# Second feed-forward and MLP by a seven-product block scheme over tokens and rows, with weight sums made by adding loads

## Chip, cores, metric

One core of a Trainium2 chip runs the whole kernel in one launch. The metric is device time in microseconds; a run is one execution, and the time given is a median over runs.

## What is computed

Two transformer blocks follow each other on 512 tokens of 1024 features, in float32. The two parts that the change touches are, cut from the reference:

```python
def swiglu(h, w_gu, w_down):            # first block, second feed-forward: w2_gu, w2_down, D_FF = 2816
    a, b = jnp.split(h @ w_gu, 2, axis=-1)
    return (jax.nn.silu(a) * b) @ w_down

h = modulate(rms_norm(x, g_ffn2[l]), sh3, sc3)
x = x + 0.5 * gt3[:, None, :] * swiglu(h, w2_gu[l], w2_down[l])

def squared_relu_mlp(xn, w_up, w_down): # second block, last part: w_up 1024 x 4096, w_down 4096 x 1024
    return jnp.square(jax.nn.relu(xn @ w_up)) @ w_down

x = x + squared_relu_mlp(rmsnorm(x, norm_mlp[l]), w_up[l], w_down[l])
```

Around them stand a first feed-forward, two mixers and a cross-attention.

## The kernel before

**Layout.** Activations are kept with features on the 128 partitions and the 512 tokens along a row: `x` and `h` are 8 tiles of 128 x 512. Weights are loaded from memory in pieces of 128 x 1024 float32 (512 KB) that the host has laid out in the order of use.

**Products in three passes.** Each float32 operand is split into a rounded part `hi` and a rest `lo`. `new_weights` (line 144) takes a raw piece from a ring of `N_RAW` = 4 buffers, makes `hi` on ScalarE (L151, a copy) and `lo` on VectorE (L152, a subtraction) in a ring of `N_WHL` = 6 `whl` buffers. `mm3` (line 156; the matmul is L160) then issues hi·hi, hi·lo and lo·hi for each row tile into one bank. `split_x` (L203, L204) does the same for activations, which live in a pool of 61 tiles of 128 x 512.

**Stages.** `linear` (line 166) makes one block of 128 columns for all 512 tokens: 8 row tiles, so 24 matmuls with 512 moving columns. `ffn` (line 609) calls it twice for each of 22 tiles of the hidden layer (gate and up), applies tanh and two multiplications (L617 to L619), splits the result into `G`, and between groups of up products runs `down` over 6 tiles of `G` (18 matmuls and one residual addition, L212, for each of the 8 output tiles). `mlp` (line 1251) does so for 32 tiles with L1258 and a square, and with `down` over 8, 8, 6 and 6 tiles (L211). The last 4 tiles go through `res_halves` (line 223), token half by token half with 256 moving columns, so that the next norm can start. The first products of a stage are also done in two token halves (`nhalf`).

**What sets the order.** The text is unrolled; a planner orders each engine's instructions before the run, by their place in the text (earlier is more urgent), by when its own model has their inputs ready, and by when a buffer is free. On the chip each engine takes its list in order, with semaphores. Loads are on SP's queue (L137), each due when a `raw` buffer comes free. There are 8 banks: 6 for `ps()`, 2 for `psx()`. `FIRST` names the weight pieces of the next stage, of which `N_AHEAD` = 1 is split ahead. GpSimd (POOL) does some memsets and issues no loads.

## Time and profile before

| | us |
|---|---|
| runs (3) | 2134.97, 2133.66, 2133.18; median 2133.66 |
| profiled execution | 2137.62 |
| its span, on which all rows stand | 2135.8 |
| granted clock of TensorE, mean | 0.996 |

The page's engines: PE is TensorE's matmuls, PEld its weight loads, DVE VectorE, ACT ScalarE, POOL GpSimd, SP the engine that issues the loads. The ends of matmuls are modelled, so a matmul's pace is read as a stretch divided by the count, not from its mean duration.

### The profile page before, as it was taken

The page shows a single profiled execution, that of the slowest core. Times are in us where ns is not written, and L with a number is a line of the kernel's source. Part 1 is how long each engine was busy: PE and PEld are TensorE (multiplying, and loading weights), DVE is VectorE, ACT ScalarE, POOL GpSimd, SP SyncE. Part 2 cuts the span into 40 slices and gives each one's busy share as a digit, 9 for nine tenths or more (in the row PEclk, how much of TensorE's full clock was granted, in tenths as well). Part 3 has the DMA queues.
Part 4 walks back from the last instruction along what each step waited for, and adds up shares of the span by engine and source line. Part 5 has one row for each costly group of instructions (what it writes and reads, how often), then busy time and mean ns, then how long its engine had stood idle before and what let it go on. Part 6 is the DMA issues. An engine that isn't in the chain of part 4 may idle for free.

```text
span 2135.8 us, 28122 instructions
## 1 busy us (share of the span) xinstructions
PE 2108.9 (99%) x10866; PEld 1767.4 (83%) x10866; DVE 1285.3 (60%) x2644; ACT 802.1 (38%) x1396; POOL 3.7 (0%) x14
## 2 busy tenths in 40 slices
PE   7999999999999999999999999999999999999998
PEld 6888888897777788898888889788889898888887
DVE  6866656588766333473434349889798565343445
ACT  4422222256554322242222225446554444232222
POOL 0000000000000000000000000000000000000000
PEclk9999999999999999999999999999999999999999
DMA  8855555444322233432423232231232313332321
GB/s 303 288 182 186 168 174 166 134 143 130 119 61 79 89 94 94 138 96 72 118 74 112 82 122 81 78 109 40 70 99 82 117 57 102 90 98 81 97 89 40
DMA packets 80278, 243.03 MB, mean 114 GB/s; under 512 B 9104, under 2 KB 14864, under 8 KB 80144
## 3 DMA queue, kind: packets, MB, share of 16 engines
q1 hardware_dynamic: 75536, 234.94, 35.3%
q10 hardware_dynamic: 4608, 6.29, 0.8%
q8 instruction: 86, 1.41, 0.3%
q14 instruction: 48, 0.39, 0.1%
HBM read 232.81 MB, written 8.39 MB: 113 GB/s over the span
## 4 chain that ended last, share of the span: by engine, by line
PE 96%; DVE 2%; ACT 1%; DMA 1%; issue 0%; SPq 0%; DVEq 0%; ACTq 0%
PE p L160 86%; PE x L979 1%; PE p L595 1%; PE x L160 1%; PE x L935 1%; PE x L745 1%; PE x L1037 1%; PE p L602 1%; PE x L920 1%; PE x L734 1%; PE x L302 1%; PE x L322 0%; DMA raw<-in_w_ada 0%; PE x L703 0%; DMA a<-in_memT 0%; ACT a L647 0%
## 5 line engine op out<-in xcount | busy, mean ns | idle before, releaser
L160 PE MATMUL p<-a,whl 128*128 128x512 f32 (+1 forms) x8736 | 1852.2, 371 | 3.3 <-ACT a L557 1.7
L160 PEld LDWEIGHTS p<-a,whl 128*128 128x128 f32 x8736 | 1504.1, 188 | 302.5 <-issue 8.0
L151 ACT CAST whl<-raw 128x1024 fp32r<-128x1024 f32 (+1 forms) x354 | 356.8, 1010 | 762.8 <-PE p L160 551.0
L152 DVE TENSOR_TENSOR whl<-raw,whl 128x1024 fp32r<-128x1024 f32 (+1 forms) x354 | 416.1, 1176 | 152.7 <-ACT whl L151 151.5
L212 DVE SCALAR_TENSOR_TENSOR a<-p,mods,a 128x512 f32<-128x512 f32 (+1 forms) x104 | 64.2, 625 | 83.8 <-PE p L160 83.5
L211 DVE TENSOR_TENSOR a<-a,p 128x512 f32<-128x512 f32 (+1 forms) x96 | 52.4, 553 | 100.5 <-PE p L160 100.2
L618 DVE SCALAR_TENSOR_TENSOR a<-a,p 128x512 f32<-128x512 f32 x44 | 30.2, 687 | 98.3 <-ACT a L617 98.3
L617 ACT ACTIVATE a<-p 128x512 f32<-128x512 f32 x44 | 26.3, 598 | 166.2 <-PE p L160 166.2
L619 DVE TENSOR_TENSOR a<-a,p 128x512 f32<-128x512 f32 x44 | 30.3, 688 | 92.5 <-PE p L160 92.2
L204 DVE TENSOR_TENSOR a<-a 128x512 fp32r<-128x512 f32 x109 | 74.7, 688 | 9.7 <-ACT a L203 9.6
L160 PE MATMUL p<-whl,a 128*128 128x256 f32 (+1 forms) x576 | 75.9, 286 | 0.0
L203 ACT CAST a<-a 128x512 fp32r<-128x512 f32 x109 | 67.0, 618 | 18.3 <-DVE a L1187 6.8
L160 PEld LDWEIGHTS p<-whl,a 128*128 128x128 f32 x576 | 71.3, 188 | 2.6 <-issue 2.2
L1258 DVE SCALAR_TENSOR_TENSOR a<-p,a 128x512 f32<-128x512 f32 x32 | 22.1, 692 | 84.5 <-PE p L160 84.5
L289 ACT ACTIVATE q<-a 128x256 f32<-128x256 f32 x120 | 48.5, 414 | 59.4 <-DVE a L211 28.3
L502 DVE CUSTOM_DVE_ANT_0 raw<-raw,a,ct 128x512 f32<-128x512 f32 x56 | 42.0, 750 | 38.1 <-DMA raw<-in_w_ada 37.4
L291 DVE TENSOR_TENSOR q<-q 128x256 f32<-128x256 f32 x90 | 37.8, 421 | 8.5 <-ACT q L289 7.4
L502 DVE CUSTOM_DVE_ANT_0 raw<-raw,a,part 128x512 f32<-128x512 f32 x56 | 42.0, 750 | 1.2
L722 ACT ACTIVATE a<-a,s 128x256 f32<-128x256 f32 (+1 forms) x64 | 30.0, 470 | 21.2 <-DVE s L717 12.5
L595 PE MATMUL p<-a,raw 128*128 128x256 f32 x80 | 21.6, 426 | 11.8 <-ACT a L549 11.8
L1013 DVE TENSOR_TENSOR a<-a 128x256 f32<-128x256 f32 x64 | 26.4, 419 | 7.2 <-PE x L967 7.1
L1012 ACT COPY a<-a 128x256 f32<-128x256 f32 x64 | 24.7, 411 | 13.3 <-DVE a L1014 12.1
(233 smaller groups left out, 1340.0 us busy)
## 6 DMA issues: line engine op xcount, KB each, us to landing
raw<-in_w_gu SPq DMA_DIRECT2D x88, 512.0 KB, 3.7
raw<-in_w_in SPq DMA_DIRECT2D x86, 512.0 KB, 3.6
raw<-in_w_ada SPq DMA_DIRECT2D x56, 512.0 KB, 4.1
raw<-in_w_down SPq DMA_DIRECT2D x64, 384.0 KB, 3.0
raw<-in_w_up SPq DMA_DIRECT2D x32, 512.0 KB, 3.5
raw<-in_w_down SPq DMA_DIRECT2D x28, 512.0 KB, 3.5
a<-in_w_ada SPq DMA_DIRECT2D x32, 256.0 KB, 4.9
raw<-in_w_out SPq DMA_DIRECT2D x16, 512.0 KB, 3.5
```

Of the source, the lines that this page charges most:

```text
L151: self.nc.scalar.copy(hi[:, ks, :], src)
L152: self.nc.vector.tensor_sub(lo[:, ks, :], src, hi[:, ks, :].bitcast(F32))
L160: self.nc.tensor.matmul(out, lw[k][a], rx[k][b], start=k == 0 and i == 0, stop=k == n - 1 and i == 2)
L203: self.nc.scalar.copy(hi, src)
L204: self.nc.vector.tensor_sub(lo, src, hi.bitcast(F32))
L211: return self.nc.vector.tensor_add(x, x, p)
L212: return self.nc.vector.scalar_tensor_tensor(x, p, gt(j), x, ALU.mult, ALU.add)
L289: nc.scalar.activation(q, x[k], AF.Square, scale=s)
L291: nc.vector.tensor_add(q, accs[i][0], q)
L502: nc.vector.tensor_tensor_reduce(out=t, in0=t, in1=self.cact[i], op0=ALU.mult, op1=ALU.add, scale=0.5, scalar=acc, accum_out=dst)
L595: nc.tensor.matmul(p, w[k], full[k], start=k == 0, stop=k == KT - 1)
L619: nc.vector.tensor_mul(th, th, pb)
```

## The change

In the second feed-forward and the MLP the products with the up weights are done on two by two blocks: rows of the weights in two halves (4 row tiles each), tokens in two halves of 256, and two column groups `c1` and `c2` of 256. Seven products of 128x128 weights with 256 moving columns replace the eight that the plain way needs. `twist` makes the sums of halves of `h` once a stage and splits them; in part they overwrite the second token half of `h`. The sums of weight blocks are made in the raw buffer: `load_q` loads a block of 4 row tiles by 256 columns on SP, and `add_q` lets GpSimd issue a load that adds another block to it, after the buffer has been split for the product before. Signs are carried so that only additions of weights are needed. `unit` holds 4 banks, and its last product is returned to be issued later, inside the next unit (`before`) or in `down` (`between`). The down products go through `res_full` over 4 tiles of `G` (2 in the last group of the feed-forward). The first 2 (feed-forward) or 4 (MLP) hidden tiles are still made by `linear`. The ring of raw buffers gets 5 entries and the pieces shrink from 1088 to 1024 columns, for which the 272-column pieces of the second mixer are cut into four.

```diff
-N_RAW = 4
+N_RAW = 5
...
-    "mix2": [("w_in_2", 0, 4, 3840, 272), ("w_in_2", 512, 4, 3840, 272), ("w_in_2", 0, 4, 3584, 256)],
+    "mix2": [("w_in_2", 0, 2, 3840, 272), ("w_in_2", 256, 2, 3840, 272), ("w_in_2", 512, 2, 3840, 272)],
...
+    def load_q(self, *q):
+        t = self.rawp.tile([128, 1024], F32, tag="raw", name="raw")[:, 0:1024]
+        self.nc.sync.dma_start(t, self.quarter(*q))
+        return t
+
+    def add_q(self, t, *q):
+        self.nc.gpsimd.dma_start(t, self.quarter(*q), accum_op=ALU.add)
+
+    def split_q(self, src):
+        t = self.whlp.tile([128, 2, 1024], F32R, tag="whl", name="whl")
+        hi, lo = (t[:, i, 0:1024] for i in range(2))
+        self.nc.scalar.copy(hi, src)
+        self.nc.vector.tensor_sub(lo, src, hi.bitcast(F32))
+        hi, lo = (u.rearrange("p (k c) -> p k c", k=4) for u in (hi, lo))
+        return [(hi[:, k, :], lo[:, k, :]) for k in range(4)]
+
+    def twist(self, h):
+        nc = self.nc
+        t1, n2, t3, t4 = [], [], [], []
+        a = slice(0, 256)
+        b = slice(256, 512)
+
+        def part(hi, lo, src, sl=slice(0, S)):
+            nc.scalar.copy(hi[:, sl], src)
+            nc.vector.tensor_sub(lo[:, sl], src, hi[:, sl].bitcast(F32))
+            return hi[:, sl], lo[:, sl]
+        for k in range(4):
+            f1, f2, w1, w2 = (self.T() for _ in range(4))
+            for f, (hi, lo) in ((f1, h[k]), (f2, h[k + 4])):
+                nc.vector.tensor_add(f, hi.bitcast(F32), lo.bitcast(F32))
+            nc.vector.tensor_sub(w2[:, a], f1[:, a], f1[:, b])
+            t1.append(part(h[k][0], h[k][1], w2[:, a], b))
+            nc.vector.scalar_tensor_tensor(w1[:, a], w2[:, a], -1.0, f2[:, b], ALU.mult, ALU.subtract)
+            nc.vector.tensor_sub(w1[:, b], f2[:, b], f1[:, b])
+            nc.vector.scalar_tensor_tensor(w2[:, b], w1[:, a], -1.0, f2[:, a], ALU.mult, ALU.subtract)
+            hi, lo = part(self.T(F32R), self.T(F32R), w1)
+            n2.append((hi[:, a], lo[:, a]))
+            t3.append((hi[:, b], lo[:, b]))
+            if k % 2 == 0:
+                q = self.T(F32R), self.T(F32R)
+            t4.append(part(q[0], q[1], w2[:, b], (a, b)[k % 2]))
+        return self.cut(h[0:4], 0, 256), self.cut(h[4:8], 0, 256), self.cut(h[4:8], 256, 512), t1, n2, t3, t4
+
+    def product(self, bank, w, x, first=False):
+        for i in range(2):
+            for k in range(4):
+                for n, (a, b) in enumerate(((0, 0), (0, 1), (1, 0))):
+                    self.nc.tensor.matmul(bank[:, i * 256:i * 256 + 256], w[k][a][:, i * 128:i * 128 + 128], x[k][b],
+                                          start=first and i == 0 and k == 0 and n == 0, stop=k == 3 and n == 2,
+                                          skip_group_check=True)
+
+    def unit(self, name, c1, c2, tw, evac, before):
+        nc = self.nc
+        b11, b21, b22, t1, n2, t3, t4 = tw
+        y = self.load_q(name, 0, c1)
+        A, B, C, D4 = self.ps(), self.ps(), None, None
+        self.product(A, self.split_q(y), b11, True)
+        self.add_q(y, name, 0, c2)
+        s = self.T()
+        nc.scalar.copy(s, A)
+        z = self.load_q(name, 512, c1)
+        self.product(B, self.split_q(z), b21, True)
+        nc.vector.tensor_add(s, s, B)
+        evac(0, 0, s)
+        x = self.load_q(name, 512, c2)
+        D4 = self.ps()
+        self.product(D4, self.split_q(x), t4, True)
+        self.add_q(x, name, 0, c2)
+        C = self.ps()
+        self.product(C, self.split_q(x), t1, True)
+        self.add_q(x, name, 0, c1)
+        self.product(A, self.split_q(x), n2)
+        self.add_q(x, name, 512, c1)
+        u2 = self.T()
+        nc.scalar.copy(u2, A)
+        if before:
+            before()
+        self.product(A, self.split_q(y), t3)
+        u3, n21 = self.T(), self.T()
+        nc.scalar.copy(u3, A)
+        nc.vector.tensor_add(n21, u3, D4)
+        evac(1, 0, n21)
+        nc.vector.tensor_add(u3, u3, C)
+        evac(1, 1, u3)
+
+        def last():
+            self.product(C, self.split_q(x), b22)
+            nc.vector.tensor_add(u2, u2, C)
+            evac(0, 1, u2)
+        return last
...
-    def res_full(self, name, r0, g, gt, c=None):
-        for c0 in range(0, D, 256) if c is None else [c]:
-            wt = self.weights(name, r0, 4, c0, 256)
-            for i in range(0, 256, 128):
+    def res_full(self, name, r0, g, gt, c=None, between=None):
+        n = 1024 // len(g)
+        for c0 in range(0, D, n) if c is None else [c]:
+            wt = self.weights(name, r0, len(g), c0, n)
+            for i in range(0, n, 128):
...
+                if between:
+                    between()
+                    between = None
...
+    def ffn_blocks(self, h, wgu, wdown, gt, after):
...
+        tw = self.twist(h)
...
+            def evac(blk, hf, t):
+                if blk == 0:
+                    th = self.T()
+                    nc.scalar.activation(th, t, AF.Tanh, scale=0.5)
+                    nc.vector.scalar_tensor_tensor(t, th, 1.0, t, ALU.add, ALU.mult)
+                part[blk, hf] = t
+                if (1 - blk, hf) not in part:
+                    return
+                t, n = part.pop((0, hf)), part.pop((1, hf))
+                nc.vector.scalar_tensor_tensor(t, t, -1.0, n, ALU.mult, ALU.mult)
+                self.split_pair(G, f, hf, t)
...
+        for f in range(2, 22, 2):
+            late = self.unit(wgu, f * 128, D_FF + f * 128, tw, evac_of(f), late)
+            n = {4: 4, 8: 4, 12: 4, 16: 4, 20: 2}.get(f, 0)
+            if n:
+                down(done, n, late)
+                done, late = done + n, None
...
-        for f0, nf in ((0, 8), (8, 8), (16, 6), (22, 6), (28, 4)):
...
+        for f in range(4):
+            up(f)
+        tw = self.twist(h)
+        for f in range(4, 32, 4):
+            late = self.unit("w_up_2", f * 128, f * 128 + 256, tw, evac_of(f), None)
+            self.res_full("w_down_2", (f - 4) * 128, [G.pop(i) for i in range(f - 4, f)], None, None, late)
```

`split_pair` splits each 256-column half of a bank into `hi` and `lo` of two tiles of `G`, so four small copies and subtractions take the place of two large ones. In the MLP, `evac` is the comparison with zero and the scaling on VectorE (a minimum with zero for the negated block) and the square on ScalarE.

## Rows read from the trace of the kernel before

**Rows 1.** The page of the kernel before: busy time, share of the span and instructions of each engine, and the chain of work that ended last, by engine and by line (shares of the span).

```profile
PE 2108.9 (99%) x10866; PEld 1767.4 (83%) x10866; DVE 1285.3 (60%) x2644; ACT 802.1 (38%) x1396; POOL 3.7 (0%) x14
PE 96%; DVE 2%; ACT 1%; DMA 1%; issue 0%; SPq 0%; DVEq 0%; ACTq 0%
PE p L160 86%; PE x L979 1%; PE p L595 1%; PE x L160 1%; PE x L935 1%; PE x L745 1%; PE x L1037 1%; PE p L602 1%; PE x L920 1%; PE x L734 1%; PE x L302 1%; PE x L322 0%; DMA raw<-in_w_ada 0%; PE x L703 0%; DMA a<-in_memT 0%; ACT a L647 0%
```

**Rows 2.** Busy time of each engine, the instructions in brackets, in two stretches: the second feed-forward (938 to 1288 us) and the MLP (1771 to 2112). After the engines: granted clock, share of the 16 DMA engines, GB/s.

```profile
core 0: us, PE busy (x) PEld busy (x) DVE busy (x) ACT busy (x) POOL busy (x), PEclk, DMA share, GB/s
938.00:1288.00 350.00, 350.00 (x1643) 289.09 (x1642) 154.67 (x201) 101.02 (x144) 1.43 (x6) 1.00 0.32 96
1771.00:2112.00 341.00, 341.00 (x1547) 279.35 (x1545) 142.75 (x173) 101.62 (x135) 0.00 (x0) 1.00 0.28 85
```

**Rows 3.** Who waited for whom in the MLP's stretch: us in total, times, longest.

```profile
ACT whl L151 <- PE p L160: 224.4, 62, 4.7
DVE a L1258 <- PE p L160: 84.5, 31, 3.3
```

**Rows 4.** The same for SP's queue of loads, over the whole span.

```profile
SPq L137 <- DVE whl L152: 1470.8, 289, 27.8
```

**Rows 5.** Busy time by stretch (columns as in rows 2): 200 us inside the second feed-forward in which all matmuls have 512 moving columns.

```profile
1000.00:1200.00 200.00, 200.00 (x864) 161.74 (x863) 80.50 (x92) 50.66 (x64) 0.00 (x0) 1.00 0.32 95
```

**Rows 6.** The same for the matmuls of line 160 alone (us, PE, PEld, clock, DMA share, GB/s), in two stretches in which all of them have 256 moving columns.

```profile
core 0: us, PE busy (x) PEld busy (x), PEclk, DMA share, GB/s
921.20:931.90 10.70, 10.70 (x90) 10.67 (x91) 1.00 0.35 117
...
1754.20:1763.80 9.60, 9.60 (x81) 9.60 (x81) 1.00 0.34 109
```

**Rows 7.** Groups of instructions in the stretch of rows 5, shapes kept apart: line, engine, operation, tiles, shapes, count, busy us, mean ns of one, idle time before and what ended it.

```profile
L152 DVE TENSOR_TENSOR whl<-raw,whl 128x1024 fp32r<-128x1024 f32 x24 | 29.4, 1226 | 8.3 <-ACT whl L151 8.3
L151 ACT CAST whl<-raw 128x1024 fp32r<-128x1024 f32 x24 | 25.2, 1049 | 62.1 <-PE p L160 45.8 <-issue 16.3
L212 DVE SCALAR_TENSOR_TENSOR a<-p,mods,a 128x512 f32<-128x512 f32 x16 | 12.0, 751 | 30.9 <-PE p L160 30.9
L618 DVE SCALAR_TENSOR_TENSOR a<-a,p 128x512 f32<-128x512 f32 x12 | 8.3, 689 | 42.3 <-ACT a L617 42.3
L619 DVE TENSOR_TENSOR a<-a,p 128x512 f32<-128x512 f32 x12 | 8.3, 688 | 36.3 <-PE p L160 36.3
L204 DVE TENSOR_TENSOR a<-a 128x512 fp32r<-128x512 f32 x12 | 8.2, 685 | 0.0
L617 ACT ACTIVATE a<-p 128x512 f32<-128x512 f32 x12 | 7.2, 599 | 49.6 <-PE p L160 49.6
```

**Rows 8.** The same inside the MLP, 1850 to 2050 us.

```profile
L1258 DVE SCALAR_TENSOR_TENSOR a<-p,a 128x512 f32<-128x512 f32 x19 | 13.1, 692 | 53.5 <-PE p L160 53.5
L211 DVE TENSOR_TENSOR a<-a,p 128x512 f32<-128x512 f32 x19 | 13.1, 689 | 50.6 <-PE p L160 50.6
```

**Rows 9.** The page's groups, VectorE and ScalarE on 256 columns (columns as in rows 7).

```profile
L291 DVE TENSOR_TENSOR q<-q 128x256 f32<-128x256 f32 x90 | 37.8, 421 | 8.5 <-ACT q L289 7.4
L1013 DVE TENSOR_TENSOR a<-a 128x256 f32<-128x256 f32 x64 | 26.4, 419 | 7.2 <-PE x L967 7.1
L1012 ACT COPY a<-a 128x256 f32<-128x256 f32 x64 | 24.7, 411 | 13.3 <-DVE a L1014 12.1
```

**Rows 10.** Busy time by stretch (columns as in rows 2), at the head of the two stages.

```profile
938.00:966.00 28.00, 28.00 (x192) 25.84 (x191) 19.23 (x31) 12.76 (x20) 0.00 (x0) 1.00 0.35 105
1764.00:1793.00 29.00, 29.00 (x174) 25.67 (x174) 16.49 (x33) 10.75 (x18) 0.00 (x0) 1.00 0.37 110
```

**Rows 11.** The same near the start of the kernel, where TensorE had gaps; the granted clock is the first number after the engines.

```profile
11.00:18.00 7.00, 6.24 (x16) 5.02 (x17) 2.33 (x2) 5.70 (x11) 0.00 (x0) 1.00 1.02 395
18.00:24.50 6.50, 4.75 (x23) 3.75 (x22) 3.18 (x9) 4.09 (x12) 0.00 (x0) 1.00 0.77 261
24.50:31.00 6.50, 6.50 (x33) 6.50 (x33) 5.18 (x22) 3.34 (x10) 0.00 (x0) 0.50 0.94 305
```

**Rows 12.** POOL in order of time: start us, duration us, line, operation, tile, idle time before and what ended it.

```profile
1248.88 0.54 POOL L1074 MEMSET a<- 128x512 f32 x1 [831.61 <-PE p L160]
1269.55 0.52 POOL L858 MEMSET a<- 64x512 f32 x1 [19.16 <-PE p L160]
```

**Rows 13.** The page's DMA issues: queue, count, KB each, median us from issue to landing.

```profile
raw<-in_w_gu SPq DMA_DIRECT2D x88, 512.0 KB, 3.7
raw<-in_w_up SPq DMA_DIRECT2D x32, 512.0 KB, 3.5
a<-in_memT SPq DMA_DIRECT2D x4, 256.0 KB, 7.7
```

More of the change, by code (lines that the diff above doesn't have):

```diff
@@ L87, in __init__ @@
         self.off = {n: 0 for n in W_SIZES}
+        self.packed = {}
         def pool(name, bufs, **kw):
@@ L134, in raw @@
             self.off[name] += 128 * n * ncol
-            t = self.T() if spread else self.rawp.tile([128, 1088], F32, tag="raw", name="raw")
+            t = self.T() if spread else self.rawp.tile([128, 1024], F32, tag="raw", name="raw")
             t = t[:, 0:n * ncol]
@@ L139, in raw, with quarter @@
         return out
+    def quarter(self, name, r0, c0):
+        if (name, r0, c0) not in self.packed:
+            self.packed[name, r0, c0] = self.off[name]
+            self.units[name].append((r0, 4, c0, 256))
+            self.off[name] += 512 * 256
+        o = self.packed[name, r0, c0]
+        return self.w[name][o:o + 512 * 256].rearrange("(p f) -> p f", p=128)
+    def load_q(self, *q):
+        t = self.rawp.tile([128, 1024], F32, tag="raw", name="raw")[:, 0:1024]
+        self.nc.sync.dma_start(t, self.quarter(*q))
+        return t
@@ L144, in new_weights @@
     def new_weights(self, name, r0, nk, c0, ncol):
-        t = self.whlp.tile([128, 2, 1088], F32R, tag="whl", name="whl")
+        t = self.whlp.tile([128, 2, 1024], F32R, tag="whl", name="whl")
         hi, lo = (t[:, i, 0:nk * ncol].rearrange("p (k c) -> p k c", k=nk) for i in range(2))
@@ L186, in tok_unit @@
         wt = []
-        for k in range(0, 8, 4):
-            wt += self.weights(name, k * 128, 4, c0, n)
+        nk = 4 if n <= 256 else 2
+        for k in range(0, 8, nk):
+            wt += self.weights(name, k * 128, nk, c0, n)
         for b in range(h[0][0].shape[-1] // 128):
@@ L490, in ada_raw @@
         if t is None:
-            t = self.rawp.tile([128, 1088], F32, tag="raw", name="raw")
+            t = self.rawp.tile([128, 1024], F32, tag="raw", name="raw")
         t = t[:, 0:nk * 128]
@@ L639, in ffn, with evac_of, down, split_pair @@
         self.res_halves(wdown, 18 * 128, [G[f] for f in range(18, 22)], gt, after)
+    def ffn_blocks(self, h, wgu, wdown, gt, after):
+        nc = self.nc
+        G = {}
+        for f in range(2):
+            pa = self.linear(wgu, f * 128, h)
+            pb = self.linear(wgu, D_FF + f * 128, h)
+            th = self.T()
+            nc.scalar.activation(th, pa, AF.Tanh, scale=0.5)
+            nc.vector.scalar_tensor_tensor(th, th, 1.0, pa, ALU.add, ALU.mult)
+            nc.vector.tensor_mul(th, th, pb)
+            G[f] = self.split_x(th)
+        tw = self.twist(h)
+        def evac_of(f):
+            part = {}
+            def evac(blk, hf, t):
+                if blk == 0:
+                    th = self.T()
+                    nc.scalar.activation(th, t, AF.Tanh, scale=0.5)
[6 more added lines that the diff above has]
+                self.split_pair(G, f, hf, t)
+            return evac
+        def down(f0, nf, late):
+            self.res_full(wdown, f0 * 128, [G.pop(f) for f in range(f0, f0 + nf)], gt, None, late)
+        late, done = None, 0
+        for f in range(2, 22, 2):
[4 more added lines that the diff above has]
+                done, late = done + n, None
+        self.res_halves(wdown, 18 * 128, [G[f] for f in range(18, 22)], gt, after)
+    def split_pair(self, G, f, hf, t):
+        sl = slice(hf * 256, hf * 256 + 256)
+        for i in range(2):
+            if f + i not in G:
+                G[f + i] = self.T(F32R), self.T(F32R)
+            hi, lo = (u[:, sl] for u in G[f + i])
+            src = t[:, i * 256:i * 256 + 256]
+            self.nc.scalar.copy(hi, src)
+            self.nc.vector.tensor_sub(lo, src, hi.bitcast(F32))
     def rope(self, p, cos, sin):
@@ L1260, in up, with evac_of, evac @@
             G[f] = self.split_x(t)
-        def down(f0, nf):
-            g = [G.pop(f) for f in range(f0, f0 + nf)]
-            for j in range(KT):
-                self.res_add(j, self.linear("w_down_2", j * 128, g, f0 * 128), slice(0, S), None)
-        nxt = 0
-        for f0, nf in ((0, 8), (8, 8), (16, 6), (22, 6), (28, 4)):
-            while nxt < min(32, f0 + nf + 2):
-                up(nxt)
-                nxt += 1
-            if f0 < 28:
-                down(f0, nf)
+        def evac_of(f):
+            def evac(blk, hf, t):
+                t3 = t.rearrange("p (a c) -> p a c", a=2)
+                r = rb[:, hf * 256:hf * 256 + 256].unsqueeze(1).to_broadcast([128, 2, 256])
+                nc.vector.scalar_tensor_tensor(t3, t3, 0.0, r, ALU.min if blk else ALU.max, ALU.mult)
+                nc.scalar.activation(t, t, AF.Square)
+                self.split_pair(G, f + 2 * blk, hf, t)
+            return evac
+        for f in range(4):
[4 more added lines that the diff above has]
+            self.res_full("w_down_2", (f - 4) * 128, [G.pop(i) for i in range(f - 4, f)], None, None, late)
         self.res_halves("w_down_2", 28 * 128, [G[f] for f in range(28, 32)], None, after)
```

2 lines of the change are left out of this document (1 added, 1 removed).

## The prediction

> **What bounds the kernel now.** I read the page's busy line and its chain first, then busy time by stage, then the pace of matmuls inside a stage, then what the weight splits and the loads wait for. TensorE is busy for nearly the whole span and is nearly the whole chain that ended last, most of it on the one line of `mm3` [rows 1]. So time goes where matmul time goes. In both changed stages TensorE is busy without a gap, VectorE under half and ScalarE under a third of the stretch, at full granted clock [rows 2]. The splits of weights wait for TensorE to give a `whl` buffer back [rows 3], and the loads on SP's queue wait for the splits to give a `raw` buffer back [rows 4]: both are early. A change that takes matmul time out of these stages shortens the kernel until something else is late.
>
> **What is removed: one product in eight.** Two 256-column units together hold 4 column blocks of 8 row tiles. Before, that is 4 × 24 = 96 matmuls with 512 moving columns; after, 7 products of 24 = 168 with 256. The pace at 512 is 200.00 / 864 = 231.5 ns [rows 5]. At 256 moving columns it is in existing stretches 10.70 / 90 = 118.9 and 9.60 / 81 = 118.5 ns [rows 6]; I take 118.5. A unit goes from 22.22 to 19.91 us, 2.31 less. The half-width costs 2.4% a column and eats a sixth of the eighth. There are 10 units in the feed-forward and 7 in the MLP: 23.1 + 16.2 = **39.3 us off TensorE**. The first 4 column products of each stage, and all products with `w_down`, keep their count and shape: nothing.
>
> In those 256-wide stretches weight loading is busy 10.67 of 10.70 us [rows 6], against 161.74 of 200 at 512 [rows 5]. The Trainium skill, "Perfetto Trace Analysis", section Identifying the Most-Contended Engine, says matmul busy time is a bad measure and to judge TensorE by MFU and by LDWEIGHTS busy share. By that rule the change moves TensorE from a load share of 81% to one of 100%, with 168 loads for 96. The trace disagrees on what follows: loads overlap, and the pace of 118.5 ns already contains them. I keep 118.5 and make the other reading a rival.
>
> **What is added on ScalarE and VectorE.** Splits: 7 a unit for 4, so 30 and 21 more, each 1.05 us on ScalarE and 1.23 on VectorE [rows 7]. Per unit also 3 adds of a bank on VectorE (0.69 each, as L619) beside 2 copies (0.60, as L617), and one add of a copied bank to another. Residual additions: the feed-forward goes from 24 to 40 full-width ones, the MLP from 32 to 56, at 0.75 and 0.69 us [rows 7, 8]. For VectorE in the feed-forward that is 154.67 + 36.9 + 27.6 + 12 + the twist (18.3, below), some 250 of 327 us; in the MLP 142.75 + 25.8 + 19.3 + 16.6 + 18.3, some 223 of 325 us [rows 2, 7]. ScalarE comes to about half. Neither becomes the bound over a stage. TensorE covers all of it while it is fed; if that cover went, splits alone would be worth 51 × 1.23 = 63 us.
>
> **The twist, at the head of each stage.** Per pair of tiles VectorE does 3 operations of 512 columns (0.69, L204) and 6 of 256 (0.42 [rows 9]): 4.6 us, four times 18.3. They need the whole `h`; the fourth product (`t4`) needs all four rounds. TensorE's cover is the first 4 column products and the two products on plain blocks. In the 28 us after `h` begins to be complete in the feed-forward, VectorE is already busy 19.23, so 8.8 are free; at the MLP's head 16.49 of 29, so 12.5 [rows 10]. The rest is idle time of TensorE: **9.5 us** and **5.8 us**. `t1` overwrites the second half of `h`, so it waits for the last of the plain products; that falls inside. Bounds: 0, if the splits of `y` and `z` come first and the backlog is worked off later, and 14 and 8, if they queue behind the twist on VectorE. After such a gap the clock can be low: near the start, where TensorE had gaps, a stretch of 6.5 us was granted 0.50 [rows 11], the 1.2 GHz level; that is worth 3.3 us a time (half of 6.5). I take half of one, 1.5, bounds 0 and 6.6.
>
> **Hand-overs through a bank.** Bank A is copied between two products that both write it. In the feed-forward the postponed last product of the unit before stands between them in every second unit; in the MLP nothing does. TensorE waits for a ScalarE copy, 0.60 us: 7 × 0.6 = **4.2**, bounds 0 (the planner puts `w_down` matmuls there) and 14 (each copy stands behind two splits). In the feed-forward, `down` at f = 4, 8, 12, 16 needs tiles whose last part comes from the postponed product: 0.69 + 0.60 + 0.69 + 0.69 + 3 × 0.42 = 3.9 us after it, against a product (2.84) and six matmuls (1.39) of cover. That just fits, but one split ahead on VectorE adds 1.23: I take **4** for the four, bounds 0 and 8.
>
> **The loads that add.** No row shows one. They read the buffer they write, and are issued from POOL's queue, 4 a unit, each behind the split of its buffer; the next split of that buffer stands in ScalarE's and VectorE's queues behind it, and whatever those queues hold after it waits too. POOL otherwise does a few memsets in this stage, one of which sat until 1248.88 for a tile [rows 12]; adds queued behind it would wait as long, but it is issued where a tile is due to be free, so I cost that at nothing. SP gets one load less a unit. Below, an add costs what a load of 512 KB does, 3.5 us; above, twice the slowest row, 2 × 7.7 [rows 13]. It moves the bytes of a plain load and reads as many again, so I take 6, nearer to the plain load. The Trainium skill, "DMA: Bandwidth & Descriptors", section Anatomy of one DMA, fits 2.0 us plus bytes / 436e3 to loads from this queue, an estimate of 3.2 us for 512 KB; it says nothing on adding ones, and no run here shows either. By it the term below would be nought as well.
>
> Is 6 us early enough? With six `whl` buffers the first split of `x` can start when the tile six before is released: right behind another unit that is 6 × 2.84 = 17.1 us ahead of its product. The third product on `x` comes 5.7 later; in 22.8 us must fit three splits (6.8) and two adds, so an add may take **8.0 us**. Behind a `down` three tiles of 5.56 stand in the ring and an add may take 12. So at 6 the term is **0**.
>
> The first loads of the next mixer come in four pieces instead of two and one buffer more lets loads run earlier; both lie under matmuls that are there already. I cost them at nothing, bounds −1 and +2.
>
> **Sum**, on the profiled execution: 39.3 − 9.5 − 5.8 − 1.5 − 4.2 − 4 = 14.3 us less, a span of 2135.8 − 14.3 = 2121.5, and 2123.3 with the 1.8 us around it (2137.62 was measured for 2135.8). The median of the runs is 4.0 below that execution: 2133.66 − 14.3 = **2119.4**. With the terms at their lower bounds 2133.7 − 39.3 − 1 is 2093; at their upper, 39.3 − 50.6 − 2, it is 2147.
>
> **Rivals.**
> (a) *The adds are late.* Place: the third and fourth product on `x`. Price: past 8.0 us two adds a unit are uncovered in the five units that directly follow another, past 12 in the other twelve too. It decides from 5 × 2 × (T − 8.0) = 14.3, T = 9.4 us. At 12 the kernel takes 2119 + 40 = 2159, at 14 some 2119 + 60 + 48 = 2227. For it: nothing bounds an add's rate from above, and queues behind a waiting split are in order. Against: plain loads land in 3.5 and DMA engines are a third busy in these stages [rows 2]. Chance 0.15.
> (b) *VectorE's queue eats it all.* At some 75% busy, with pieces of 1.23 us, each hand-over waits for one or two splits: 14 + 8 + 22 + 3 = 47 lost, or little less. Time 2130 to 2141. For: the load above. Against: the planner has other matmuls to put there. Chance 0.14, over half of it within 0.2% of before.
> (c) *Weight loading binds at half width.* If each of the 168 loads took its 161.74 / 863 = 187 ns [rows 5] in turn, a unit takes 31.5, 9.3 more than before: 2133.7 + 17 × 9.3 = 2291. Against: the pace of rows 6. Chance 0.02.
> That the change doesn't do what it says, seven products for eight, I exclude: 168 matmuls a unit stand in the text.
>
> **Numbers.** The forecast has 0.69; alone it runs from 2097 to 2129. Range 2097 to 2145: it takes in (b) and the start of (a). A difference of 0.2% (4.3 us) is about what can be told from none. Faster by more: 0.69; within: 0.09; slower: 0.22, from (a), (c) and a third of (b).
>
> **What would show it.** Matmuls of 256 at 118 to 119 ns in the units; TensorE idle of some 10 and 6 us at the two heads, with the twist on VectorE before it; short waits for the bank copy in the MLP; the splits of `x` waiting for POOL's loads, but not TensorE for them. Adds of over 8 us with TensorE idle ahead of the second and third product on `x` would make it wrong, as would no idle time at the heads, which would give some 2104.

## The result, and the profile after

The kernel after took **2152.51 us** (median of 4 runs, 2151.67 to 2154.02), the kernel before 2134.26 on the same chip: ratio **1.0087** [1.0069, 1.0104], slower by 0.9%, where 2119.4 and faster was forecast. The profiled executions are 2154.02 and 2137.62, 16.4 apart, and the stages below add up to that. A stage is measured from the second norm-broadcast matmul ahead of it to the first one behind it, so the same two events bound it in every kernel:

| | up to second feed-forward | second feed-forward | second mixer and cross-attention | MLP |
|---|---|---|---|---|
| before | 937.78 | 363.59 | 469.75 | 356.80 |
| after | 939.46 | 377.79 | 469.59 | 357.57 |

The forecast was −23.1 gross in the feed-forward and −16.2 in the MLP. The stages came out at +14.2 and +0.8.

The page of the kernel after answers to [rows 1]: busy time, the chain by engine, the splits of the units' blocks (four of the seven in a unit are of added blocks), and the adding loads (count, KB each, us to landing).

```profile
PE 2092.6 (97%) x12066; PEld 1811.9 (84%) x12066; DVE 1428.9 (66%) x2915; ACT 892.4 (41%) x1562; POOL 62.4 (3%) x82
...
PE 86%; DMA 6%; DVE 3%; ACT 3%; issue 2%; SPq 0%; ACTq 0%; DVEq 0%; POOLq 0%
...
L163 DVE TENSOR_TENSOR whl<-raw,whl 128x1024 fp32r<-128x1024 f32 x119 | 144.7, 1222 | 177.3 <-ACT whl L162 177.3
L162 ACT CAST whl<-raw 128x1024 fp32r<-128x1024 f32 x119 | 123.2, 1049 | 257.3 <-DMA raw<-in_w_up 118.0
...
L157 POOL DMA_DIRECT2D raw<-in_w_gu x40 | 34.7, 866 | 812.0 <-DVE whl L163 794.4
...
raw<-in_w_gu POOLq DMA_DIRECT2D x40, 512.0 KB, 5.4
raw<-in_w_up POOLq DMA_DIRECT2D x28, 512.0 KB, 5.4
```

TensorE fell from 96% of the chain to 86%, and DMA, ScalarE and VectorE took its place. Splits of added blocks (L162, L163) stood idle for loads, where those of [rows 3] waited for TensorE. No engine is full but TensorE.

Busy time by stretch, columns as in [rows 2, 10]: the two stages from bound to bound, then the head of each.

```profile
core 0: us, PE busy (x) PEld busy (x) DVE busy (x) ACT busy (x) POOL busy (x), PEclk, DMA share, GB/s
939.46:1317.25 377.79, 355.29 (x2446) 328.94 (x2445) 245.25 (x378) 163.49 (x258) 34.93 (x45) 0.96 0.53 129
1786.84:2144.41 357.57, 343.95 (x2148) 308.77 (x2146) 221.19 (x353) 143.30 (x221) 23.33 (x27) 0.98 0.45 114
...
938.00:966.00 28.00, 22.12 (x170) 20.60 (x168) 22.26 (x47) 10.58 (x20) 1.73 (x2) 0.94 0.33 68
...
1806.00:1830.00 24.00, 17.39 (x85) 14.57 (x85) 22.16 (x45) 9.68 (x19) 0.00 (x0) 0.86 0.33 88
```

TensorE lost time in two ways. It is idle for 22.5 us in the feed-forward and 13.6 in the MLP, where 3.5 are idle in the kernel before too (in the last norm). And it is busy for 355.3 and 344.0 us with work that takes 340.5 and 336.7 in a kernel that has no other gaps (`e12_neither`, below): 14.8 and 7.2 us more, which agrees with a mean clock of 0.96 and 0.98. So about two fifths of the loss, against `e12`, is a clock that was at its lower level after some of the gaps.

The pace that carries the gross gain is right. Line 201 (the matmul of `product`) in the MLP, columns as in [rows 6]:

```profile
1904.95:1919.14 14.19, 14.19 (x120) 13.98 (x119) 1.00 0.55 154
```

14.19 / 120 = 118.3 ns. A period of one unit and one `down` in the MLP lasts 42.07 us (1904.95 to 1947.02) without a gap, as foreseen (19.9 + 22.2). The MLP's whole loss lies ahead of it, in its first two units.

**A pair of units in the feed-forward** (1102.13 to 1168.84) takes 66.7 us with its `down`, where 2 × 19.9 + 22.2 = 62.0 are needed. In order of time, POOL, then ScalarE, then TensorE (start us, duration; in brackets the idle time before and what ended it):

```profile
1123.23 0.86 POOL L157 DMA_DIRECT2D raw<-in_w_gu  x1 [9.02 <-DVE whl L163]
1131.24 0.86 POOL L157 DMA_DIRECT2D raw<-in_w_gu  x1 [7.16 <-DVE whl L163]
```
```profile
1128.64 1.05 ACT L162 CAST whl<-raw 128x1024 fp32r<-128x1024 f32 x1 [3.64 <-DMA raw<-in_w_gu]
...
1136.61 1.04 ACT L162 CAST whl<-raw 128x1024 fp32r<-128x1024 f32 x1 [3.07 <-DMA raw<-in_w_gu]
1137.56 1.04 ACT L258 CAST whl<-raw 128x1024 fp32r<-128x1024 f32 x1
1138.51 0.58 ACT L231 COPY a<-p 128x512 f32<-128x512 f32 x1
```
```profile
1101.97 34.76 PE L201 MATMUL p<-a,whl 128*128 128x256 f32 x288
1139.14 4.53 PE L201 MATMUL p<-a,whl 128*128 128x256 f32 x24 [2.40 <-ACT a L231]
1143.46 4.25 PE L267 MATMUL p<-a,whl 128*128 128x512 f32 x17
```

The add issued at 1131.24 lets its split start at 1136.61, 5.4 us later. TensorE did not wait for that split. It waited for the copy of bank A (L231), which came behind the split and one `w_down` split in ScalarE's list. Without the 3.07 us of waiting both would have been done before TensorE came to the end of its 288 matmuls at 1136.73. The next 24 matmuls start 4.32 us ahead of their successor, 180 ns each, at a mean granted clock of 0.64 (part of them at the 1.2 GHz level), so the gap of 2.4 us cost 24 × (180 − 118.3) = 1.5 us more. Not every gap did so: in the pair before, the same wait was 1.98 us long and the clock stayed at 1.00.

```profile
1036.00:1102.10 66.10, 63.37 (x436) 57.86 (x435) 39.50 (x50) 26.26 (x36) 6.90 (x8) 1.00 0.59 144
1072.52 3.13 PE L201 MATMUL p<-a,whl 128*128 128x256 f32 x24 [1.98 <-ACT a L231]
1139.14:1143.46 4.32, 4.32 (x24) 4.32 (x25) 4.30 (x5) 2.47 (x3) 0.00 (x0) 0.64 0.85 282
```

From one add's issue to the next on the same buffer it is 8.0 us: 5.4 to landing and 2.6 for the split on two engines.

The Trainium skill, "PSUM — Partial Sum Buffer", section Engine vs sequencer instructions, states that the queues of ScalarE and VectorE are strict FIFO. These rows agree: a copy that needs no load stood behind a split that waited for one.

**At the head of the MLP** the same on VectorE (ScalarE's split first):

```profile
1802.04 1.05 ACT L162 CAST whl<-raw 128x1024 fp32r<-128x1024 f32 x1 [5.89 <-DMA raw<-in_w_up]
```
```profile
1803.12 1.23 DVE L163 TENSOR_TENSOR whl<-raw,whl 128x1024 fp32r<-128x1024 f32 x1 [4.92 <-ACT whl L162]
1804.30 0.69 DVE L312 TENSOR_TENSOR a<-a 128x512 fp32r<-128x512 f32 x1
1804.91 0.68 DVE L1423 SCALAR_TENSOR_TENSOR a<-p,a 128x512 f32<-128x512 f32 x1
1805.51 1.22 DVE L163 TENSOR_TENSOR whl<-raw,whl 128x1024 fp32r<-128x1024 f32 x1
1806.95 0.69 DVE L312 TENSOR_TENSOR a<-a 128x512 fp32r<-128x512 f32 x1 [0.22 <-ACT a L311]
1807.56 0.68 DVE L183 TENSOR_TENSOR a<-a 128x512 f32<-128x512 f32 x1
```

VectorE stands idle for 4.92 us before the split of an added block (its add went out at 1796.51), and the operations of the last plain tiles (L312, L1423) come behind it. The twist (L183 on) begins at 1807.56, 20.7 us into the stage; TensorE has the unit's two products on plain blocks until 1808.69 and then waits for pieces of the twist (L177 is its split on ScalarE):

```profile
1802.88 5.82 PE L201 MATMUL p<-a,whl 128*128 128x256 f32 x48
1811.81 0.74 PE L201 MATMUL p<-a,whl 128*128 128x256 f32 x4 [3.12 <-ACT a L177]
```

### The profile page after: what moved, and what is told of

Its sections match the earlier page's. It is cut to its first block, busy times and chain, and to the rows that moved or that the text cites. A ratio compares the mean times of both kernels' runs of the same rounds, so it can differ in the third digit from the quotient of the medians.

```text
span 2152.2 us, 31078 instructions
## 1 busy us (share of the span) xinstructions
PE 2092.6 (97%) x12066; PEld 1811.9 (84%) x12066; DVE 1428.9 (66%) x2915; ACT 892.4 (41%) x1562; POOL 62.4 (3%) x82
## 4 chain that ended last, share of the span: by engine, by line
PE 86%; DMA 6%; DVE 3%; ACT 3%; issue 2%; SPq 0%; ACTq 0%; DVEq 0%; POOLq 0%
PE p L267 67%; PE p L201 8%; DMA raw<-in_w_gu 5%; DMA raw<-in_w_up 1%; PE x L1144 1%; DVE whl L163 1%; PE p L707 1%; ACT whl L162 1%; PE x L267 1%; PE x L1100 1%; PE x L910 1%; PE x L1202 1%; PE p L714 1%; PE x L1085 1%; PE x L899 1%
## 5 line engine op out<-in xcount | busy, mean ns | idle before, releaser
L267 PE MATMUL p<-a,whl 128*128 128x512 f32 (+1 forms) x7080 | 1482.6, 366 | 5.6 <-ACT a L669 1.7
L267 PEld LDWEIGHTS p<-a,whl 128*128 128x128 f32 x7080 | 1195.4, 189 | 232.7 <-issue 10.1
L258 ACT CAST whl<-raw 128x1024 fp32r<-128x1024 f32 (+2 forms) x278 | 283.0, 1023 | 394.6 <-PE p L267 255.3
L259 DVE TENSOR_TENSOR whl<-raw,whl 128x1024 fp32r<-128x1024 f32 (+2 forms) x278 | 330.3, 1191 | 124.4 <-ACT whl L258 123.7
L201 PE MATMUL p<-a,whl 128*128 128x256 f32 x2856 | 365.4, 288 | 31.0 <-ACT a L177 13.5
L201 PEld LDWEIGHTS p<-a,whl 128*128 128x128 f32 x2856 | 356.3, 195 | 42.4 <-ACT a L177 15.3
L163 DVE TENSOR_TENSOR whl<-raw,whl 128x1024 fp32r<-128x1024 f32 x119 | 144.7, 1222 | 177.3 <-ACT whl L162 177.3
L162 ACT CAST whl<-raw 128x1024 fp32r<-128x1024 f32 x119 | 123.2, 1049 | 257.3 <-DMA raw<-in_w_up 118.0
L157 POOL DMA_DIRECT2D raw<-in_w_gu x40 | 34.7, 866 | 812.0 <-DVE whl L163 794.4
L729 ACT ACTIVATE a<-p 128x512 f32<-128x512 f32 x22 | 13.2, 598 | 83.8 <-PE p L267 83.8
L312 DVE TENSOR_TENSOR a<-a 128x512 fp32r<-128x512 f32 x61 | 41.6, 685 | 5.2 <-ACT a L311 5.1
L803 ACT CAST a<-a 128x256 fp32r<-128x256 f32 x96 | 34.2, 404 | 24.4 <-DVE a L779 23.5
```

The costliest lines, as they stand in the source:

```text
L157: self.nc.gpsimd.dma_start(t, self.quarter(*q), accum_op=ALU.add)
L162: self.nc.scalar.copy(hi, src)
L163: self.nc.vector.tensor_sub(lo, src, hi.bitcast(F32))
L201: self.nc.tensor.matmul(bank[:, i * 256:i * 256 + 256], w[k][a][:, i * 128:i * 128 + 128], x[k][b], start=first and i == 0 and k == 0 and ...
L258: self.nc.scalar.copy(hi[:, ks, :], src)
L259: self.nc.vector.tensor_sub(lo[:, ks, :], src, hi[:, ks, :].bitcast(F32))
```

## The experiments

Stage times of every kernel's profile, in us, and the device time (medians of several runs for after, `e9` and `e11`, else one run; the kernel before ran at 2134.15, 2135.32, 2134.49 and 2134.75 beside the four batches e1–e4, e5–e8, e9–e11, e12):

| | device | second feed-forward | MLP |
|---|---|---|---|
| before | 2134.26 | 363.59 | 356.80 |
| after | 2152.51 | 377.79 | 357.57 |
| e1_no_add | 2114.54 | 350.28 | 348.14 |
| e2_own_bank | 2161.53 | 392.34 | 349.75 |
| e3_no_twist | 2127.67 | 373.61 | 340.18 |
| e4_more_plain | 2152.14 | 375.35 | 360.99 |
| e5_reload | 2120.35 | 356.84 | 347.99 |
| e6_early_twist | 2145.36 | 378.29 | 348.81 |
| e7_mlp_alone | 2127.75 | 362.91 | 348.15 |
| e8_down_each | 2187.34 | 414.30 | 357.75 |
| e9_twist_first | 2130.53 | 362.90 | 345.93 |
| e10_copy_first | 2141.93 | 374.41 | 348.89 |
| e11_both | 2133.12 | 374.92 | 340.16 |
| e12_neither | 2095.40 | 340.48 | 340.20 |

The MLP's times of `e9` and `e11` are some 3.0 us too short to be set beside the others. Both put all four plain products first, and 23 matmuls of the stage move ahead of its first bound: between the two norm-broadcast pairs there lie 74 matmuls of 256 columns where every other kernel has 51, and 10.2 us for 7.2 (`after`, `e9`, `e11`; the rows count the norm's matmuls too):

```profile
1779.64:1786.84 7.20, 7.20 (x61) 7.14 (x60) 6.31 (x20) 2.49 (x5) 0.86 (x1) 1.00 0.35 59
1762.02:1772.23 10.21, 10.11 (x83) 9.85 (x82) 9.44 (x31) 3.48 (x7) 1.00 (x1) 1.00 0.17 26
1772.70:1782.89 10.19, 10.07 (x83) 9.82 (x82) 9.44 (x31) 3.48 (x7) 0.86 (x1) 1.00 0.18 27
```

Counted alike, `e9` has 348.9 and `e11` 343.1.

The feed-forward of before repeats within 0.7 us (363.59, 362.91, 362.90). The stretch up to it wanders by 5 us between kernels that do not differ there, so I compare stages. Two theories were tried. **S**: in the feed-forward the splits that wait for adding loads stand in ScalarE's and VectorE's lists ahead of work that TensorE needs. **H**: at the heads the twist starts too late. The rivals were costs of the bank copies, and of the extra work as such.

**Adding loads and twist, each out and both out: `e1`, `e3`, `e12`.**

```diff
 # e1: add_q
-        self.nc.gpsimd.dma_start(t, self.quarter(*q), accum_op=ALU.add)
+        self.quarter(*q)
 # e3: twist (e12: both edits)
-        for k in range(4):
-            f1, f2, w1, w2 = (self.T() for _ in range(4))
...
+        t1 = n2 = t3 = t4 = self.cut(h[0:4], 256, 512)
```

> The adding loads are left out, so the products use unsummed blocks; everything else stays, with the same matmuls. Theory H (the heads of the stages are lost to the twist on VectorE and the low clock after it) and Q (in the feed-forward a copy of bank A stands in ScalarE's list behind a split that waits for an adding load): the steady pair of units falls from 66.7 us to 62.1 to 62.7, the heads keep most of their loss, the kernel takes 2128 to 2136. Rival L (the adding loads are themselves what all of the loss is due to, heads too): 2110 to 2118.

> The twist is left out: the products that need sums of halves of h use plain slices of h, so VectorE and ScalarE do none of its work. Theory H: each head gets 12 to 16 us shorter, the kernel takes 2120 to 2128, steady pairs stay at 66.7. Rival L: the heads still wait for the first unit's chain of adding loads, which has no lead there, and the kernel stays above 2140.

> Leaves out both the adding loads and the twist: the products with weight sums take the first block's weights, the products with sums of tokens take the plain second half of h. All matmuls, splits, bank copies and additions stay. Theory (the gross gain of the count is there in full, 23.1 us in the second feed-forward and 16.2 us in the MLP; what was lost went to the adding loads, with the work behind the splits that wait for them, and to the twist, and nothing to the copies of bank A by themselves): second feed-forward 363.6 - 23.1 = 340.5 us within 3, MLP 356.8 - 16.6 = 340.2 within 1.5, in all about 2094. Rival (the copies of bank A and the down products' wait for G cost something even when nothing in ScalarE's list waits for a load, as the prediction's hand-over terms of 4 and 4.2 us said): second feed-forward 344.5 or more, MLP 344 or more, in all 2102 or more.

`e1` came out where rival L put it, `e3` in the range of theory H, but with 4.2 us won at the feed-forward and 17.4 at the MLP. Neither theory alone had the loss right. `e12` came out as its theory said. With both out the stages take 340.48 and 340.20: 23.1 and 16.6 below before. The gross gain is there to a tenth of a microsecond per unit, with every split, bank copy, added bank and `down` in place:

```profile
935.20:1275.67 340.47, 340.47 (x2446) 318.71 (x2445) 233.13 (x343) 160.57 (x246) 1.28 (x6) 1.00 0.26 82
1745.66:2085.87 340.21, 336.72 (x2149) 303.48 (x2147) 210.69 (x317) 141.64 (x209) 0.00 (x0) 1.00 0.23 76
```

(Feed-forward and MLP of `e12`, columns as above.) VectorE is busy for 233 of 340 us and costs nothing. Weight loads are busy for 94% of the stretch, against 83% in [rows 2]. By the rule of the Trainium skill, "Perfetto Trace Analysis", section Identifying the Most-Contended Engine, that is less headroom; the whole gain came all the same.

What the two parts cost over `e12`:

| us lost | second feed-forward | MLP |
|---|---|---|
| twist alone (e1) | 9.8 | 7.9 |
| adding loads alone (e3) | 33.1 | 0.0 |
| both (after) | 37.3 | 17.4 |

So the adding loads are the main loss in the feed-forward: 33.1 us alone, 27.5 on top of the twist. In the MLP, where a `down` of 22 us stands between any two units, they cost nothing by themselves, and 9.4 us on top of the twist. Set against `e12` matmul by matmul, each stage from its first bound, the kernel after is 22.1 us late in the feed-forward once the first two units are done, and each pair after that adds some 4 us (`e3`: 15.2 and some 4). In the MLP it is 10.9 us late behind the first unit (`e1`: 7.6) and 17.4 behind the second, where one wait of 3.53 us for the copy of bank A stands (at 1871.47; clock 0.83 from 1870 to 1890). So most of the 9.4 us is a late copy; the twist itself begins only 1.6 us later than in `e1`. In `e3` TensorE waited in the feed-forward 10.1 us for the copy and 9.5 us for the waiting splits themselves. With the twist out, the 12 tiles that it holds stay free as well, which no run takes apart.

**Does the loss grow with the load's duration? `e5`.**

```diff
 # add_q
-        self.nc.gpsimd.dma_start(t, self.quarter(*q), accum_op=ALU.add)
+        self.nc.sync.dma_start(t, self.quarter(*q))
```

> Each adding load is replaced by a plain load over the same buffer, on SP's queue, so the chain of load and split stays and only the load is shorter (some 3.3 us to landing for 5.4); the products use unsummed blocks. Theory S (ScalarE's list in the feed-forward stands behind splits that wait for the chain, so the loss grows with a link's length): the feed-forward stage, 377.8 us with adding loads and 350.3 with none, takes 356 to 368; the MLP 350 to 357. Rival (any wait in the chain costs the same, or the loss is the added reading): 374 or more.

The plain loads over the buffer land in 3.4 us, and the feed-forward takes 356.8, in the range of theory S (the MLP's 348.0 is 2 us below its range): 16.4 above `e12`, with the twist in, where after is 37.3 above. The waits of ScalarE's splits for loads there are 65.2 us in all, 100.7 after. A link in the same place that is some 2 us shorter loses less than half; of the 16.4 the twist by itself has 9.8. The edit also takes the loads from GpSimd's queue to SP's and spares the reading of the buffer, so it does not tell these apart from the length.

**Is it the hand-over through bank A? `e2`, `e10`, `e8`.** `e2` gives the sixth product a bank of its own. `e10` makes the planner put the last split of `x` behind the first copy of bank A. `e8` puts a `down` of two tiles behind every unit.

```diff
 # e2: unit
-        self.product(A, self.split_q(y), t3)
+        E = self.ps()
+        self.product(E, self.split_q(y), t3, True)
...
-        nc.scalar.copy(u3, A)
+        nc.vector.tensor_add(u3, u2, E)
 # e10: unit, last()
-        nc.scalar.copy(u2, A)
+        copied = nc.scalar.copy(u2, A)
-            self.product(C, self.split_q(x), b22)
+            self.product(C, self.split_q(x, copied), b22)
 # e8: ffn_blocks
-            n = {4: 4, 8: 4, 12: 4, 16: 4, 20: 2}.get(f, 0)
...
+            if f > 2:
+                down(f - 4, 2, late)
+                late = None
```

> The product with t3 goes to a bank of its own, and its sum with the copied bank is made by one addition on VectorE in place of a second copy: TensorE no longer waits for the copy of bank A. The results are the same sums. Theory Q: the steady pair in the feed-forward goes from 66.7 to 62.1 to 63, its 2.4 us gap and the slow matmuls after it go, the MLP loses its one gap of 3.5; 2128 to 2136. Rival L: TensorE comes to the next product that waits for an adding load, the pair stays at 65 or more and the kernel above 2145.

> The changed kernel with one more rule for the planner: the split for a unit's last product stands behind that unit's first copy of bank A in ScalarE's list. Same sums, loads and matmuls. Theory S with Q: the copy no longer waits for an adding load, the steady pair of units in the feed-forward goes from 66.7 to 62.1 to 64 and the stage from 377.8 to 358 to 368. Rival (the chain itself is too long, TensorE then waits for the weights of the last product or for G): 374 or more.

> In the feed-forward a down over 2 tiles follows each unit from the second on, in place of one over 4 after every second unit, so that each unit's chain of loads has as much plain work beside it; the same sums in another order of addition. Theory S: the chain of three links of 8.0 us and four splits fits under 31 us a unit, the stage goes from 377.8 to 355 to 368. Rival (the links are too slow for any order, or the doubled residual additions on VectorE take it back): 374 or more.

None of the three came out as its theory said: `e2`, `e10` and `e8` all landed on the rival's side. TensorE's waits in the feed-forward, `e2`, `e10` and `e8` in turn (us in total, times, longest):

```profile
PE p L268 <- ACT a L804: 12.4, 4, 3.7
PE p L201 <- ACT a L177: 7.7, 5, 3.0
PE p L201 <- ACT whl L162: 6.8, 5, 2.3
```
```profile
PE p L271 <- ACT a L807: 6.6, 3, 2.4
```
```profile
PE p L201 <- ACT a L231: 32.8, 8, 5.2
```

Without the hand-over (`e2`) TensorE waits for the split of `G` on ScalarE (L804) and for the waiting splits themselves: the stage is 14.6 us slower, not faster. With the copy put first (`e10`) the wait for the copy is gone, the wait for `G`'s split (L807) takes its place, and 3.4 us are won. With a `down` behind each unit (`e8`) the copy is waited for 32.8 us. The hand-over is thus where the loss shows and not, or not alone, what makes it: something else in ScalarE's list behind a waiting split becomes the wait. `e10` also brought the MLP to 348.9: its wait for the copy in the second unit is gone, and the first wait for the twist is 1.97 us instead of 3.12. `e2`, which takes the copy away, has 349.8.

**Theory S's forecast for `e8`, 355 to 368, failed by 46 us.** Rows of one unit of `e8` (POOL, ScalarE, TensorE), then the same of the MLP of the kernel after:

```profile
1091.24 0.86 POOL L157 DMA_DIRECT2D raw<-in_w_gu  x1 [10.02 <-DVE whl L163]
1113.08 1.04 ACT L162 CAST whl<-raw 128x1024 fp32r<-128x1024 f32 x1 [2.87 <-DMA raw<-in_w_gu]
1115.92 0.58 ACT L231 COPY a<-p 128x512 f32<-128x512 f32 x1
1097.27 14.34 PE L201 MATMUL p<-a,whl 128*128 128x256 f32 x120
```
```profile
1891.61 0.86 POOL L157 DMA_DIRECT2D raw<-in_w_up  x1 [4.03 <-DVE whl L163]
1914.45 1.05 ACT L162 CAST whl<-raw 128x1024 fp32r<-128x1024 f32 x1 [4.55 <-DMA raw<-in_w_up]
1919.17 0.59 ACT L231 COPY a<-p 128x512 f32<-128x512 f32 x1 [0.50 <-PE p L201]
1904.79 14.35 PE L201 MATMUL p<-a,whl 128*128 128x256 f32 x120
```

In `e8` the first add on `x` goes out 6.0 us ahead of the unit's first product, the split behind the third add starts 15.8 us after that product's start, and the copy, due after five products (14.2 us), stands behind it. In the MLP the first add goes out 13.2 us ahead, the split starts at 9.7, and the copy waits for TensorE alone. So 11 us of `down` did not give the lead that 22 us give; why it gave hardly any (5.7 us where a unit follows another directly) is not shown. `e8` also takes away the postponed product that stood between the copy and the next product in every second unit, and no run separates the two.

**The heads: `e4`, `e6`, `e7`, `e9`, `e11`.** `e4` makes twice as many plain tiles ahead of the first unit, and in the MLP puts a first `down` among them. `e6` puts the twist's rounds ahead of the last plain evacuations in the text; `e7` is `e6` with the feed-forward as before; `e9` is `e7` with the rounds ahead of all plain evacuations; `e11` does that in both stages and has `e10`'s rule.

```diff
 # e4: mlp (ffn_blocks alike: range(2) becomes range(4))
-        for f in range(4):
+        for f in range(8):
             up(f)
+            if f == 5:
+                self.res_full("w_down_2", 0, [G.pop(i) for i in range(4)], None, None)
...
-        for f in range(4, 32, 4):
+        for f in range(8, 32, 4):
 # e9: mlp (e6: two up(f) stand ahead of the steps)
+        step, finish = self.twist(h)
+        ps = [self.linear("w_up_2", f * 128, h) for f in range(4)]
+        for k in range(4):
+            step(k)
         for f in range(4):
-            up(f)
-        tw = self.twist(h)
+            up(f, ps[f])
+        tw = finish()
 # e7, e9
-                self.ffn_blocks(h, "w2_gu", ...
+                self.ffn(h, "w2_gu", ...
```

> Two more hidden tiles of the feed-forward and four more of the MLP are made the plain way ahead of the blocks (one unit less in each), and the MLP's first down products come ahead of the first unit. Theory H: the twist and the first chain lie under these products; each head gets 12 to 18 us shorter and one unit's gain of 2.3 is given up, 2118 to 2130. Rival L: the first unit's chain starts no earlier relative to its products, the kernel stays above 2145.

> The twist's four rounds stand in the text ahead of the last plain products' evacuations, only the part that overwrites h after them; same sums. Theory H (a buffer for the twist is given out in the order of the text, so it began only when the plain products were evacuated): the MLP stage goes from 357.6 to 340 to 346, the feed-forward from 377.8 to 366 to 376, as far as the chain of loads lets it. Rival (the twist's 18 us on VectorE delay splits and evacuations wherever they stand): the MLP stays above 352.

> As e6, with the second feed-forward as in the kernel before, so the blocks are in the MLP alone. Theories H and S: the feed-forward takes 362 to 365, the MLP 340 to 346, the kernel 2115 to 2124, faster than both. Rival: the MLP above 352 and the kernel 2130 or more.

> As e7 (blocks in the MLP alone), with the twist's four rounds in the text ahead of the evacuation of all four plain products, so that no buffer that the twist needs stands behind one of theirs. Theory H: in e7 the twist began when the second plain tile had been evacuated; now it begins with h, the MLP stage goes from 348.2 to 340 to 345 us and the kernel takes 2112 to 2124, faster than before by 0.5 to 1.0%. Rival (the twist now holds back the evacuations and with them the banks): 348 or more, the kernel as e7.

> e10's rule and e9's early twist in both stages, blocks in both. If both theories hold and add up: the feed-forward 348 to 360, the MLP 340 to 346, the kernel 2098 to 2118, faster than both. Rival (what was shown for one stage does not hold with the other, or the chain takes it back): the feed-forward above 370 and the kernel 2120 or more.

More plain work (`e4`) does not help, as its rival said: the MLP is at 361.0 with one unit fewer, 18.1 above what its six units would allow (356.8 − 6 × 2.31). The twist started only when the last plain tile had been evacuated, however many there were. Text order moves it: with the rounds ahead of the last two tiles it starts 10 us into the stage for 20.7, and the MLP takes 348.8 (`e6`) and 348.2 (`e7`), between theory and rival. Ahead of all tiles (`e9`) it starts before the bound, and the MLP takes 348.9, counted alike: nothing more, as the rival said, and the two profiled executions, 2127.75 and 2127.89, agree. With the copy's order as well (`e11`) it is 343.1, 2.9 above `e12`. Three edits that touch different things (`e2`, `e6`, `e10`) thus each win 8 to 9 us in the MLP, and `e10` does so with the twist as late as before (20.5 us); so `e6` by itself does not show that the start of the twist is what was lost. In the feed-forward the early twist wins nothing. There it now holds the plain evacuations back (`e11`, TensorE):

```profile
948.73 4.41 PE L212 MATMUL p<-a,whl 128*128 128x256 f32 x36
966.25 12.23 PE L212 MATMUL p<-a,whl 128*128 128x256 f32 x89 [13.11 <-DVE a L775]
```

With two tiles of plain work as cover, one order loses at the twist and the other at the evacuation. So `e11` missed its forecast in the feed-forward and as a whole.

`e9`, blocks in the MLP alone, beats both kernels, by less than was forecast: 2130.53 (7 runs, 2126.61 to 2132.63), ratio to before **0.9976** [0.9965, 0.9987]. `e11` is level with before: 2133.12, 0.9989 [0.9979, 1.0]. Both show 472.7 us for the second mixer and cross-attention, where the others show 469.6 to 470.5; those are the 3 us of the MLP's products that moved ahead of the bound. By the stages, `e9`'s feed-forward without blocks and `e11`'s MLP together would be some 6 us lower than `e9`; that was not run.

## Why the prediction was wrong

- **What bounds the kernel, the pace, the gross gain**: right. 118.3 ns for 118.5; 23.1 and 16.6 us for 23.1 and 16.2 (`e12`). Rival (c), weight loading, is out.
- **Added work on ScalarE and VectorE under cover**: right as long as nothing waits (`e12`, VectorE 233 of 340 us, loss none). VectorE is busy for 245 and 221 us in the two stages, for the 250 and 223 worked out.
- **Twist, 9.5 and 5.8**: 9.8 and 7.9 by itself, so the size was near. In place it came with the adds, and in the MLP the two cost 17.4. The prediction had VectorE begin the twist when `h` was there and asked how much of it fitted in; its order in the list, behind waiting splits and plain evacuations, was not a term.
- **Hand-overs, 4.2 and 4**: nought by themselves (`e12`). They were priced as their own cost. With the adding loads TensorE waited for the copy 12.2 us in five waits, four of them (8.6 us) in the feed-forward, in just those units where the postponed product was to cover it.
- **The adding loads, term 0**: the step that failed. The duration was fair: 5.4 us for the 6 taken. The test was wrong in two ways. It asked for two adds before the third product on `x`, and there is a third add, for the postponed product: three links of 8.0 us are 24.0, more than the 19.9 us of a unit, so in units that follow one another its split comes due inside the next unit. And it asked whether TensorE would wait for the block. It named that whatever the queues hold behind a waiting split waits too, and then gave that no price. That was 33.1 us in the feed-forward by itself, and 27.5 and 9.4 us on top of the twist in the two stages. That the adding loads cost this is shown by leaving them out; that it happens by the lists is shown in the rows of single units, and no run freed the lists and won the time back.
- **Low clock after gaps, 1.5**: 14.8 + 7.2 us. It was taken as half of one event of 6.5 us. The low level came back after several gaps (2.29 and 2.40 us in the pairs, 3.53 in the MLP), though not after all: those of 1.98 and 1.95 us in the other two pairs left the clock at 1.00.
- **Rival (a), the adds late**: its sign was right, and the units that it named, those that directly follow another; the product it named, its price and its threshold were not. It was to decide from 9.4 us to landing, and 5.4 was enough, since TensorE waited mostly for work behind the split and only 3.0 us in the feed-forward for the split itself. With 12 us of room in the MLP it was right that nothing is lost there, as long as the twist is out.
- **Rival (b)**, VectorE full: not it. Its time of 2130 to 2141 is where `e11` came out, for other reasons.
- **Range**: 2097 to 2145 left out most of rival (a), and even the sum's own upper bound of 2147; 2152.5 lies beyond both, in the stretch of rival (a).

The sum again by stages: −23.1 − 16.6 + 37.3 + 17.4 = +15.0, as the table's 14.2 + 0.8. It closes by construction, since the last two terms are the kernel after less `e12`; it shows the sizes and tests nothing.

What stays open: what makes the 22.1 us that the feed-forward loses in its first two units, more than half of its loss, since the experiments on the order worked on the pairs or on the twist; how the lists make up the whole of the loss, as theory S held in `e5` and failed in `e8`, `e10` and `e11`; and why the copy and the split of `G` cannot both be early in the feed-forward. `e10` moved one, and no order was tried in which both stand ahead of the splits that wait, or with these splits on another engine.

## What to carry to other kernels

A wait in an in-order list is to be priced by what stands behind it, on every engine that shares the waiting step, and not only by whether the waiter's own result is late; a stage may stall with every engine but one under 70% busy. When a buffer is reused in a chain (load, split, add, split), set the whole chain, all links, against the time between two uses. Look at how far ahead of its use the chain can start: with the twist out the same loads cost 33 us where units followed one another, and nothing where 22 us of other products stood between any two. Alternating is no recipe by itself: with 11 us between (`e8`) the stage got 36.5 us slower. And when stage times are compared between orders of work, check that the same work lies between the bounds.

## What the runs showed of the hardware

- A load of 512 KB that adds into its buffer lands in 5.4 us (median of 68, 5.1 to 8.3), against 3.3 to 4.1 for plain ones of the up weights, and takes GpSimd 0.866 us to issue. The Trainium skill, "DMA: Bandwidth & Descriptors", section Anatomy of one DMA, fits 2.0 us plus bytes / 436e3 to loads from this queue, by which I estimate 3.2 us; the measured one is 2.2 longer.
- Short gaps can cost twice. After 2.4 us of idle time 24 matmuls ran at 180 ns in place of 118.3, at a mean granted clock of 0.64; after 1.98 us of it the clock stayed at 1.00. Over both stages 32.6 us of gaps, beyond those that the kernel before has, came with 22.0 us of slower matmuls.
